# A hybrid encoder trunk in which the low halves of the second batch's output weights are multiplied first, its stores are cut in two, and three pauses of the planner are changed

## The chip, the cores and the metric

One Trainium2 chip, of which the kernel uses one core. The metric is the device time of one execution in microseconds (us). The core's engines each run their own list of instructions in order: TensorE (PE in the profile) multiplies and transposes, VectorE (DVE) and ScalarE (ACT) do element work, GpSimd (POOL) a few small powers, and SyncE (SP) issues nearly all DMA transfers. An instruction that waits holds up everything behind it on its engine.

## The reference

Two independent inputs (a prompt and a sample, 512 rows of 1024 columns each, fp32) go through one encoder layer and a final norm with the same weights:

```python
mod = c_act @ w_ada + b_ada                      # six vectors of 1024 per input: sh1 sc1 g1 sh2 sc2 g2
h = rms_norm(x, norm1_g) * (1 + sc1) + sh1
q_a, k_a, v_a, q_r, k_r, v_r, g_r = split(h @ w_in)
o_a = windowed_attention(q_a, k_a, v_a, sink)    # 8 heads of 64, window 128, distance bias, a sink
y = retention(q_r, k_r, v_r, decays)             # 4 heads of 128, both directions
yn = (y - mean(y)) * rsqrt(var(y) + EPS)         # per row and head
o_r = silu(g_r) * yn
x = x + g1 * (concat(o_a, o_r) @ w_out)
h = rms_norm(x, norm2_g) * (1 + sc2) + sh2
x = x + g2 * (square(relu(h @ w_mlp1)) @ w_mlp2) # 1024 -> 4096 -> 1024
return rms_norm(x, final_g)
```

Retention is evaluated as one 512 by 512 matrix of scores per head, multiplied by a table of decays. A reference of fp32 quality is wanted, so each fp32 product is made of three matmuls in the reduced type fp32r: both operands are split into a high part (a cast) and a low part (the difference), and high by high, high by low and low by high are added up in PSUM.

## The kernel before

**Stages.** A front part computes the first norm's modulations and the attention projections of batch 0 in an order that is written out step by step. Then `run_units` goes through a list of *units*. A unit loads a block of weights (a tile of 128x1024, 512 KB) and multiplies it. The next unit's load is called one unit ahead. The first list holds batch 0's retention values and, for each of four heads, the projections q, k and gate; the second list holds the same and attention for batch 1; the third is `out_units(0)`, the output projection of batch 0, and the fourth `out_units(1)`. An output projection has two column halves `hf` of 512, each with four units `kq` of 256 rows of the weight; its products `po_b_hf_t` are four banks, one for each tile `t` of 128 rows of x. After the mixing part come the two MLP matrices in a scheme of seven products (lines 840 to 1400).

**What runs between.** Each unit yields a few times, and at each yield `between` runs background work: a stage of an attention block or a retention head (`rate` stages per yield), the norm of batch 1's x, and a step of `background_mods` (`pace` steps per yield), which is 60 reductions `jka_b` on DVE for the rest of the six modulation vectors, each over a 128x1024 tile `raw_adat` loaded by SP. A retention head (`ret_head`) does scores `prs`, their decayed copies `rsf` and split `rsc`, values `py`, transposes `pyn`, row mean and variance on DVE, a power on POOL, a scaled copy `ryn` on ACT and transposes back `pyb`. A stage that yields n is not resumed until n yields later. What comes out of this Python order is then placed on the engines by a scheduler, so neighbours in the code may end up apart.

**Batch 1's output units.** Batch 0 splits each output weight itself and keeps both halves in DRAM (`kept_wo`); batch 1 loads the kept halves, `wh_wo1_hf_kq` and `wl_wo1_hf_kq`. The low halves go into a pool `late` that is opened after the mixing part's pool has been closed and lies over its memory. So the first of them may be loaded only after the last user of the old memory, which is the last `jka_b` reduction (`jka_b_3_7`) and its read of the accumulator. When a half `hf` is done, each tile is multiplied by the gate row (`go`) and added to x (`x2`); after the second half the tile is stored to DRAM (`x2s`, 512 KB), its squares are summed (`jk2`, ACT), the reciprocal root comes from POOL (`r2`), and the tile is scaled in place. The scaling waits for the store to have landed. Tiles 0 and 2 of batch 1 are scaled by ACT, tile 1 by DVE; tile 3 goes into copies `xl` and does not wait for its store. Then come transposes `px2`, which feed the first MLP's products `px_0_0_0` and `py_0_0_n`; some of those fill gaps between the output units.

The three matmuls of a product for the output units come from `mm3_late(groups, 1)`: for a group of two tiles or one, all high by high and high by low matmuls first, and then the matmuls with the low weight.

Of the kernel before, what the change touches and what calls it, by code (L numbers as in the profile page):

```python
# [12 lines left out]
AF = mybir.ActivationFunctionType  # L13
# [19 lines left out]
def trunk_kernel(ctx, tc, x0, x1, x0_t, x1_t, params, gate2_bias, w_ada_first, w_ada_t, w_ada_gate2, w_in_first, w_in,  # L33
# [34 lines left out]
    def small(shape, name, tag="small", bufs=24):  # L68
        return work.tile(shape, F32, tag=tag, name=name, bufs=bufs)
# [57 lines left out]

    def mm3_late(groups, late):

        for ps, lhs, rhs, start, _ in groups:  # L130
            nc.tensor.matmul(ps, lhs[0], rhs[0], start=start, stop=False)  # L131
            nc.tensor.matmul(ps, lhs[late], rhs[1 - late], start=False, stop=False)  # L132
        for ps, lhs, rhs, _, stop in groups:
            nc.tensor.matmul(ps, lhs[1 - late], rhs[late], start=False, stop=stop)  # L134

# [46 lines left out]
    def last_of(engine):  # L182
        return next(i for i in reversed(nc.cur_bb.bb.instructions) if i.engine == engine)
# [226 lines left out]
    def ret_head(b, h, q_, k_, v_, sg, mix):  # L410
# [41 lines left out]
        va = small([P, NT], f"rva_{nm}")  # L452
        nc.vector.tensor_scalar(va, mv[:, :, 1], EPS, None, ALU.add)
        nb = small([P, NT], f"rnb_{nm}")
        nc.vector.tensor_scalar(nb, mv[:, :, 0], -1.0, None, ALU.mult)
        rs = small([P, NT], f"rrs_{nm}")
        nc.gpsimd.tensor_tensor(rs, va, neghalf[:, :NT], ALU.pow)
        yn = f2(f"ryn_{nm}")
        nc.gpsimd.tensor_tensor(nb, nb, rs, ALU.mult)
        for t in range(NT):  # L460
            nc.scalar.activation(yn[:, t * P:(t + 1) * P], pn[:, t * P:(t + 1) * P], AF.Identity, bias=nb[:, t:t + 1],
                                 scale=rs[:, t:t + 1])
        yield 2
        pb = aux_bank(f"pyb_{nm}")
# [64 lines left out]
    def decay_table(b, h):  # L529
        if b == 1:  # L530
            dt = mwork.tile([P, TW], F32, tag="dtab", name=f"dtab_{b}_{h}", bufs=2)
            nc.sync.dma_start(dt, kept_tables[h])
            return dt
        dt = mwork.tile([P, TW], F32, tag="dtab", name=f"dtab_{b}_{h}", bufs=2)

        nc.scalar.activation(dt, dl, AF.Copy, scale=lg[:, 0, h:h + 1])
        nc.vector.scalar_tensor_tensor(dt, dl, nlb[:, h:h + 1], dt, ALU.mult, ALU.min)
        nc.scalar.activation(dt, dt, AF.Exp)
        nc.sync.dma_start(kept_tables[h], dt)
        return dt  # L540
# [176 lines left out]
    def out_units(b, late=None):  # L717
# [14 lines left out]

        def store(t):
            r0 = b * S + t * P
            nc.sync.dma_start(x2s[r0:r0 + P, :], x2[t])

# [16 lines left out]
        def unit(hf, kq):  # L753
# [20 lines left out]
            def use(wm):  # L774
# [3 lines left out]
                for ts_ in ((0,), (1,), (2,), (3,)) if kq == 3 else ((0, 1), (2, 3)):  # L778
                    mm3_late([(banks[hf][t], [ms[k][:, i, t * P:(t + 1) * P] for i in range(2)],
                               (w[0][:, k, :], w[1][:, k, :]), kq + k == 0, kq + k == 4) for t in ts_ for k in range(2)], 1)  # L780
                    if ts_[-1] == 1:
                        yield
                if kq == 3:
                    for t in range(NT):
# [4 lines left out]
                        nc.vector.tensor_tensor(g_, banks[hf][t], gr[hf], ALU.mult)  # L789
                        nc.vector.tensor_tensor(x2[t][:, hs], x2[t][:, hs], g_, ALU.add)  # L790
                        if hf == 1 and b == 1:
                            store(t)
                            squares(hf, t)
                            if t > 0:
                                scaled(t - 1)
# [408 lines left out]
    for h in range(RH):  # L1204
        units = units + ret_units(hT[0], 0, h)
    run_units(units, 1.3, {7: lambda: extra.append(norm_x1())})
    units = attn_units(hT[1], 1) + ret_v_units(hT[1], 1)
    for h in range(RH):
        units += ret_units(hT[1], 1, h)
    run_units(units, 1.3)  # L1210
    units, norm2_0 = out_units(0)
    run_units(units, 1.0)
    flush()
# [373 lines left out]
```

## Time and profile before

| what | value |
|---|---|
| time, median of 3 runs | 1107.09 us (1106.03 to 1108.5) |
| the profiled execution | 1107.0 us, of which 1105.2 us are its span |
| TensorE busy | 1081.8 us, 98% |
| VectorE busy | 864.2 us, 78% |
| ScalarE busy | 516.0 us, 47% |
| GpSimd busy | 53.3 us, 5% |
| read and written in HBM | 160.75 MB, 71.06 MB |
| mean granted TensorE clock | 0.998 |

The profile shows one execution. Its times are counted from the span's start. A row of a timeline has the start, the duration, the engine, the line, the operation, what is written and read, and in brackets the idle time before it with what ended it. In PE's rows durations overlap: the distance between starts is the pace. A DMA row of SyncE shows when the transfer was issued; how long it took to land stands in the view of DMA issues or in the chain of waits. The stages lie at about 0 to 56 us (front), 56 to 175 (batch 0), 175 to 345 (batch 1), 345 to 430 (`out_units(0)`), 430 to 505 (`out_units(1)` and the start of the first MLP matrix); after that come the MLPs.

### The profile page before, as it was taken

The numbers are of one execution on the slowest core, as the hardware profiler recorded it, in microseconds if no ns is written. First come the engines' busy times: TensorE is split into PE (matmuls) and PEld (weight loads), VectorE is DVE, ScalarE is ACT, GpSimd is POOL, SyncE is SP. The second block draws the span as 40 slices with busy tenths as digits, with TensorE's granted clock in tenths as the row PEclk, the third lists the DMA queues.
The fourth block names the chain that finished last, engine by engine and source line by source line (L and its number), as shares of the span: only waits on it lengthen the run. The fifth ranks groups of instructions, "written<-read, shape, count | busy, mean of one in ns | idle before, by whom it ended". The sixth has DMA issues, their size and how long they took to land.

```text
span 1105.2 us, 14046 instructions
## 1 busy us (share of the span) xinstructions
PE 1081.8 (98%) x5021; PEld 889.3 (80%) x5021; DVE 864.2 (78%) x1448; ACT 516.0 (47%) x885; POOL 53.3 (5%) x63
## 2 busy tenths in 40 slices
PE   8999999999999999999999999999999999999997
PEld 5777887777888787888888888888888888888886
DVE  7979898877885787789778777786759754589786
ACT  6576676545652443474433333333443732335342
POOL 1000000010000001000000000000000000002213
PEclk9999999999999999999999999999999999999999
DMA  9888898855545698633555445552883555525504
GB/s 373 336 303 314 303 346 271 248 179 175 171 156 180 229 362 302 256 146 126 190 181 184 159 152 176 169 190 105 300 325 109 187 192 196 206 77 191 190 20 152
DMA packets 86746, 232.73 MB, mean 211 GB/s; under 512 B 8578, under 2 KB 20882, under 8 KB 86676
## 3 DMA queue, kind: packets, MB, share of 16 engines
q1 hardware_dynamic: 86084, 231.25, 60.3%
q8 instruction: 39, 0.64, 0.2%
q10 hardware_dynamic: 432, 0.57, 0.1%
q14 instruction: 31, 0.25, 0.1%
q0 software_dynamic: 160, 0.02, 0.0%
HBM read 160.75 MB, written 71.06 MB: 210 GB/s over the span
## 4 chain that ended last, share of the span: by engine, by line
PE 82%; DVE 11%; ACT 2%; DMA 2%; issue 1%; POOL 1%; POOLq 0%; DVEq 0%; ACTq 0%
PE x L1357 16%; PE px_None L940 15%; PE y L1357 12%; PE py_None L940 11%; PE po L132 2%; PE po L134 2%; PE po L131 2%; DVE jka_b L178 2%; PE po L396 2%; PE ppt L389 1%; PE psc L360 1%; PE pj_rq L131 1%; PE pj_rq L132 1%; PE pj_rq L134 1%; DVE jka_f L178 1%
## 5 line engine op out<-in xcount | busy, mean ns | idle before, releaser
L1297 DVE TENSOR_TENSOR uc_l<-ur,uc_h 128x1024 fp32r<-128x1024 f32 x56 | 68.4, 1221 | 52.7 <-ACT uc_h L1297 35.5
L1357 PE MATMUL x<-wc_l,uc_h 128*128 128x512 f32 (+1 forms) x264 | 101.0, 383 | 0.0
L1357 PE MATMUL x<-wc_h,uc_l 128*128 128x512 f32 (+1 forms) x264 | 101.0, 383 | 0.0
L1357 PE MATMUL x<-wc_h,uc_h 128*128 128x512 f32 (+1 forms) x264 | 100.9, 383 | 0.0
L1297 ACT CAST uc_h<-ur 128x1024 fp32r<-128x1024 f32 x56 | 58.8, 1051 | 77.1 <-PE x L1357 25.1
L1357 PE MATMUL y<-wc_h,uc_h 128*128 128x512 f32 x192 | 74.7, 389 | 0.0
L1357 PE MATMUL y<-wc_l,uc_h 128*128 128x512 f32 x192 | 74.7, 389 | 0.0
L1357 PE MATMUL y<-wc_h,uc_l 128*128 128x512 f32 x192 | 74.7, 389 | 0.0
L1297 ACT CAST wc_h<-w 128x1024 fp32r<-128x1024 f32 x48 | 50.5, 1051 | 48.1 <-PE x L1357 24.7
L1297 DVE TENSOR_TENSOR wc_l<-w,wc_h 128x1024 fp32r<-128x1024 f32 x48 | 58.6, 1220 | 17.6 <-ACT wc_h L1297 13.6
L1357 PEld LDWEIGHTS x<-wc_h,uc_h 128*128 128x128 f32 x264 | 49.6, 188 | 9.9 <-issue 0.2
L1357 PEld LDWEIGHTS x<-wc_l,uc_h 128*128 128x128 f32 x264 | 49.6, 188 | 9.7
L1357 PEld LDWEIGHTS x<-wc_h,uc_l 128*128 128x128 f32 x264 | 49.6, 188 | 9.6
L131 PE MATMUL po<-wh_wo,ms 128*128 128x512 f32 x128 | 50.3, 397 | 0.0
L132 PE MATMUL po<-wh_wo,ms 128*128 128x512 f32 x128 | 49.8, 392 | 0.1
L178 DVE CUSTOM_DVE_ANT_0 jka_b<-raw_adat,cb,cols 128x1024 bf16<-128x1024 f32 x38 | 48.3, 1280 | 0.2
L845 ACT CAST wc_s4h<-raw_w 128x1024 fp32r<-128x1024 f32 x16 | 16.8, 1052 | 63.1 <-PE px_None L940 44.9
L370 ACT ACTIVATE st<-st,negm 128x256 f32<-128x256 f32 (+1 forms) x64 | 35.2, 554 | 20.1 <-DVE negm L365 20.1
L1357 PEld LDWEIGHTS y<-wc_h,uc_h 128*128 128x128 f32 x192 | 36.0, 188 | 7.5
L1357 PEld LDWEIGHTS y<-wc_l,uc_h 128*128 128x128 f32 x192 | 36.0, 188 | 7.5
L1357 PEld LDWEIGHTS y<-wc_h,uc_l 128*128 128x128 f32 x192 | 36.0, 188 | 7.5
L940 PE MATMUL py_None<-hch,wc_a 128*128 128x512 f32 x120 | 39.7, 389 | 0.0
(379 smaller groups left out, 2963.0 us busy)
## 6 DMA issues: line engine op xcount, KB each, us to landing
ur<-spill SPq DMA_DIRECT2D x56, 512.0 KB, 4.4
raw_adat<-in_w_ada_t_dram SPq DMA_DIRECT2D x36, 512.0 KB, 6.4
raw_w<-in_w_mlp_dram SPq DMA_DIRECT2D x32, 512.0 KB, 3.5
spill<-s SPq DMA_DIRECT2D x64, 256.0 KB, 3.6
w<-in_w_mlp_dram SPq DMA_DIRECT2D x32, 512.0 KB, 5.0
spill<-u SPq DMA_DIRECT2D x48, 256.0 KB, 2.0
raw_ada<-in_w_ada_t_dram SPq DMA_DIRECT2D x12, 512.0 KB, 9.3
x<-in_x_dram SPq DMA_DIRECT2D x12, 512.0 KB, 7.7
```

Source lines behind the costliest of these rows:

```text
L131: nc.tensor.matmul(ps, lhs[0], rhs[0], start=start, stop=False)
L132: nc.tensor.matmul(ps, lhs[late], rhs[1 - late], start=False, stop=False)
L134: nc.tensor.matmul(ps, lhs[1 - late], rhs[late], start=False, stop=stop)
L178: nc.vector.tensor_tensor_reduce(junk(f"jka_{name}_{sec}_{kc}_{b}"), t, cb[:, b, :], 1.0, bcol[:, sec * KC + kc:sec * KC + kc + 1] if bias ...
L360: nc.tensor.matmul(psc[:, :w], qs[hh][:, isl], k_[:, s, j0 * P:j1 * P], start=(s == 0), stop=(s == 1))
L370: nc.scalar.activation(st[hh][:, :w], st[hh][:, :w], AF.Exp, bias=negm[:, hh:hh + 1], scale=0.125, accum_out=den[:, hh:hh + 1])
L389: nc.tensor.transpose(pt[:, hh * P:(hh + 1) * P], st[hh][:, jj * P:(jj + 1) * P], ident)
L396: nc.tensor.matmul(po, va[:, j0 + jj, g].rearrange("p s e -> p (s e)"), pts[jj][:, s, :], start=(jj == 0 and s == 0), stop=(jj == nj - 1 a ...
L845: nc.scalar.copy(hi, src)
L940: self.last = nc.tensor.matmul(bank[:, cs], x[:, k, :], y, start=first and k == 0 and i == 0, stop=last and k == 3 and i == 2, skip_group_ ...
L1297: last_split[:] = [nc.scalar.copy(hi, src), nc.vector.tensor_sub(lo, src, f(hi))]
L1357: nc.tensor.matmul(out, left[n][x][:, i, ts_], right[n][y][:, i, cs], start=first and i == 0 and k == 0, stop=end and i == 1 and k == 2, s ...
```

## The change

```diff
@@ mm3_late
-        for ps, lhs, rhs, start, _ in groups:
-            nc.tensor.matmul(ps, lhs[0], rhs[0], start=start, stop=False)
-            nc.tensor.matmul(ps, lhs[late], rhs[1 - late], start=False, stop=False)
-        for ps, lhs, rhs, _, stop in groups:
-            nc.tensor.matmul(ps, lhs[1 - late], rhs[late], start=False, stop=stop)
+    def mm3_late(groups, late, low_first=False):
+        def low():
+            for ps, lhs, rhs, start, stop in groups:
+                nc.tensor.matmul(ps, lhs[1 - late], rhs[late], start=start and low_first, stop=stop and not low_first)
+        if low_first:
+            low()
+        for ps, lhs, rhs, start, stop in groups:
+            nc.tensor.matmul(ps, lhs[0], rhs[0], start=start and not low_first, stop=False)
+            nc.tensor.matmul(ps, lhs[late], rhs[1 - late], start=False, stop=stop and low_first)
+        if not low_first:
+            low()
@@ ret_head
-        nc.vector.tensor_scalar(va, mv[:, :, 1], EPS, None, ALU.add)
         nb = small([P, NT], f"rnb_{nm}")
         nc.vector.tensor_scalar(nb, mv[:, :, 0], -1.0, None, ALU.mult)
+        nc.vector.tensor_scalar(va, mv[:, :, 1], EPS, None, ALU.add)
...
-        yield 2
+        yield 3
         pb = aux_bank(f"pyb_{nm}")
@@ decay_table
-        nc.scalar.activation(dt, dl, AF.Copy, scale=lg[:, 0, h:h + 1])
+        with tc.issue_after(last_of(mybir.EngineType.Activation)):
+            nc.scalar.activation(dt, dl, AF.Copy, scale=lg[:, 0, h:h + 1])
@@ out_units
-        def store(t):
+        def store(t, cs=slice(0, D)):
             r0 = b * S + t * P
-            nc.sync.dma_start(x2s[r0:r0 + P, :], x2[t])
+            nc.sync.dma_start(x2s[r0:r0 + P, cs], x2[t][:, cs])
...
-                               (w[0][:, k, :], w[1][:, k, :]), kq + k == 0, kq + k == 4) for t in ts_ for k in range(2)], 1)
+                               (w[0][:, k, :], w[1][:, k, :]), kq + k == 0, kq + k == 4) for t in ts_ for k in range(2)], 1, b == 1)
...
+                        if b == 1:
+                            store(t, hs)
                         if hf == 1 and b == 1:
-                            store(t)
                             squares(hf, t)
@@ the body
-    run_units(units, 1.3, {7: lambda: extra.append(norm_x1())})
+    run_units(units, 1.3, {3: lambda: clock.__setitem__(3, 0.8), 7: lambda: extra.append(norm_x1())}, 0.0)
...
-    run_units(units, 1.3)
-    units, norm2_0 = out_units(0)
-    run_units(units, 1.0)
+    more, norm2_0 = out_units(0)
+    run_units(units + more, 1.3)
```

In words: batch 1's output units multiply with the low weight first and the high weight after it. The `x2` tiles of batch 1 are stored in halves of 256 KB, the first after `hf` 0. Each retention head pauses three yields in place of two between its row statistics and the transposes back, and computes the negated mean before the variance. The first step of a decay table is tied behind the last ACT instruction emitted so far. The background reductions rest during the first four units and then go at 0.8 per yield (0.7 before), and batch 1's units and `out_units(0)` are one list with one rate of 1.3, so that the first output weight is called for a unit earlier. PE, ACT, DVE and POOL execute as many instructions as before; SP issues four more transfers. The order on the engines changes in many places; the three on which the prediction rests follow.

**The start of batch 1's output units, SP and PE.** On SP, `wh_`/`wl_` are loads of the kept halves, `x2s` stores of batch 0's tiles. Before:

```order
L876 DMA raw_w1_0_0_4548<-in_w_mlp1_dram 128x1024
L119 DMA wl_wo1_0_0_4408<-kept_wo0_0_3901 128x1024
L119 DMA wh_wo1_0_0_4406<-kept_wo0_0_3901 128x1024
L119 DMA wh_wo1_0_1_4416<-kept_wo0_1_3972 128x1024
L119 DMA wl_wo1_0_1_4418<-kept_wo0_1_3972 128x1024
L119 DMA wl_wo1_0_2_4488<-kept_wo0_2_4025 128x1024
L735 DMA x2s_69<-x2_0_0_4139 128x1024
L735 DMA x2s_69<-x2_0_1_4144 128x1024
L735 DMA x2s_69<-x2_0_2_4149 128x1024
L735 DMA x2s_69<-x2_0_3_4154 128x1024
L119 DMA wh_wo1_0_2_4486<-kept_wo0_2_4025 128x1024
```

Now:

```order
L119 DMA wh_wo1_0_0_4406<-kept_wo0_0_3885 128x1024
L119 DMA wh_wo1_0_1_4416<-kept_wo0_1_3973 128x1024
L741 DMA x2s_69<-x2_0_0_4154 128x1024
L119 DMA wh_wo1_0_2_4486<-kept_wo0_2_4029 128x1024
L741 DMA x2s_69<-x2_0_1_4159 128x1024
L741 DMA x2s_69<-x2_0_2_4164 128x1024
L741 DMA x2s_69<-x2_0_3_4169 128x1024
L119 DMA wl_wo1_0_0_4408<-kept_wo0_0_3885 128x1024
L119 DMA wl_wo1_0_1_4418<-kept_wo0_1_3973 128x1024
L119 DMA wl_wo1_0_2_4488<-kept_wo0_2_4029 128x1024
```

The first low half `wl_wo1_0_0` stood ahead of the four stores of batch 0's tiles, and stands behind them now. On PE the first products of these units follow directly on the last product of `out_units(0)`, now:

```order
L132 MATMUL po_0_1_3_4193<-wl_wo0_1_3_4313,ms_0_3_0_4023 128x512
L132 MATMUL po_0_1_3_4193<-wl_wo0_1_3_4313,ms_0_3_1_4026 128x512
L132 MATMUL po_1_0_0_4426<-wl_wo1_0_0_4408,ms_1_0_0_4410 128x512
L132 MATMUL po_1_0_0_4426<-wl_wo1_0_0_4408,ms_1_0_1_4413 128x512
L132 MATMUL po_1_0_1_4427<-wl_wo1_0_0_4408,ms_1_0_0_4410 128x512
L132 MATMUL po_1_0_1_4427<-wl_wo1_0_0_4408,ms_1_0_1_4413 128x512
L136 MATMUL po_1_0_0_4426<-wh_wo1_0_0_4406,ms_1_0_0_4410 128x512
```

Before, the transposes `pyb_1_3` and eight products with `wh_wo1_0_0` stood between the first of these rows and the first use of `wl_wo1_0_0`.

**The last background reduction, DVE.** `jka_b_3_7` are the two reductions on whose end the load of `wl_wo1_0_0` waits. Before:

```order
L101 TENSOR_TENSOR wl_wo0_1_3_4286<-raw_wo0_1_3_4283,wh_wo0_1_3_4285 128x1024
L425 TENSOR_TENSOR rsc_1_3_3_4263<-rsf_1_3_3_4261,rsc_1_3_3_4263 128x512
L178 ISA jka_b_3_7_0_4278,mod_s1_90<-raw_adat_35_4201,cb_85,cols_82 128x1024
L178 ISA mod_s1_90 128x1
L178 ISA jka_b_3_7_1_4304,mod_s1_90<-raw_adat_35_4201,cb_85,cols_82 128x1024
L178 ISA mod_s1_90 128x1
L768 TENSOR_TENSOR ms_1_0_0_4410<-mix_1_0_2248,ms_1_0_0_4410 128x512
```

Now:

```order
L795 TENSOR_TENSOR go_0_1_2_4388<-po_0_1_2_4192,gate_0_0_512_4279 128x512
L795 TENSOR_TENSOR go_0_1_3_4391<-po_0_1_3_4193,gate_0_0_512_4279 128x512
L796 TENSOR_TENSOR x2_0_2_4164<-x2_0_2_4164,go_0_1_2_4388 128x512
L796 TENSOR_TENSOR x2_0_3_4169<-x2_0_3_4169,go_0_1_3_4391 128x512
L183 ISA jka_b_3_7_0_4394,mod_s1_90<-raw_adat_35_4331,cb_85,cols_82 128x1024
L183 ISA mod_s1_90 128x1
L183 ISA jka_b_3_7_1_4396,mod_s1_90<-raw_adat_35_4331,cb_85,cols_82 128x1024
L183 ISA mod_s1_90 128x1
L746 SCALAR_TENSOR_TENSOR v2_0_0_4451<-ss2_0_0_2113 128x1
```

The reductions have moved behind `go_0_1_3`, which reads the last product of `out_units(0)`, and behind two additions.

**The end of batch 1's output units, ACT.** `jk2` sums squares of a tile's second half, the rows that write `x2_1_t` scale a tile, `u` belongs to the MLP. Before:

```order
L730 ACTIVATE jk2_1_1_2_4891,ss2_1_2_4404<-x2_1_2_4662 128x512
L951 COPY u_0_2_4919<-px_0_0_0_4925 128x256
L730 ACTIVATE jk2_1_1_3_4902,ss2_1_3_4405<-x2_1_3_4667 128x512
L953 COPY u_0_3_4920<-py_0_0_3_4967 128x256
L749 ACTIVATE x2_1_2_4662<-x2_1_2_4662,r2_1_2_4906 128x1024
L821 ACTIVATE hr_1_0_4981<-px2_1_0_4985,mod_s1_90,mod_a1_88 128x512
```

Now:

```order
L736 ACTIVATE jk2_1_1_2_4895,ss2_1_2_4404<-x2_1_2_4664 128x512
L958 COPY u_0_2_4923<-px_0_0_0_4929 128x256
L960 COPY u_0_3_4924<-py_0_0_3_4971 128x256
L755 ACTIVATE x2_1_2_4664<-x2_1_2_4664,r2_1_2_4910 128x1024
L736 ACTIVATE jk2_1_1_3_4906,ss2_1_3_4405<-x2_1_3_4670 128x512
L828 ACTIVATE hr_1_0_4985<-px2_1_0_4989,mod_s1_90,mod_a1_88 128x512
```

The squares of tile 3 have moved behind the scaling of tile 2, which waits for tile 2's store. On PE, the products of `py_0_0_1` and `py_0_0_3` that stood between the last output product and the transposes `px2_1_0` (16 of them) now stand ahead of the last eight pairs of products with `wh_wo1_1_3`; the transposes of `x2_1_2` and `xl_1_0` stand where they stood.

1 line of the change is left out of this document (removed).

## The prediction

> **What bounds the kernel now.** I read PE's busy time by stage first (columns: window, length, busy time and count of PE, weight loads, DVE, ACT and POOL, granted clock, DMA share, GB/s), then the view of waits for PE between 53 and 510 us (us in total, times, longest).
>
> ```profile
> 56.00:505.00 449.00, 438.93 (x2156) 361.39 (x2155) 368.49 (x819) 244.87 (x518) 19.83 (x26) 1.00 0.70 242
> 505.00:1105.00 600.00, 592.75 (x2650) 490.91 (x2648) 447.00 (x536) 236.76 (x319) 29.98 (x29) 1.00 0.51 173
> ```
>
> ```profile
> PE pyb L466 <- ACT ryn L461: 3.1, 4, 1.3
> PE px L268 <- ACT x L749: 1.4, 1, 1.4
> PE pj_rq L131 <- DVE rv L298: 1.2, 1, 1.2
> PE py L124 <- ACT rsc L424: 1.0, 1, 1.0
> PE pj_rv L131 <- DVE ks L311: 0.8, 1, 0.8
> PE pj_rv L131 <- DVE qs L338: 0.8, 1, 0.8
> PE py L940 <- ACT wc_a L845: 0.7, 1, 0.7
> PE px L268 <- DVE x L751: 0.3, 1, 0.3
> ```
>
> PE sets the end. After 505 us the change leaves PE's work as it is. Between 56 and 505 us PE idles for 449.0 - 438.9 = 10.1 us, of which these rows hold 9.3. PE's products are the same in number, so **10.1 us is the most that can be won**, and each new wait of PE is paid in full. The question is which of these waits go, and which come.
>
> **What it wins.** The two waits for `ks` and `qs` (1.6 us) lie behind the first steps of two decay tables on ACT, which the order now puts later:
>
> ```profile
> 49.69 1.98 ACT L536 ACTIVATE dtab<-dl,lg 128x896 f32<-128x896 f32 x2 [1.67 <-DVE lg L523]
> ```
>
> 1.98 us of ACT covers 1.6 us of waiting: I take all of it, with 0 as the other end. The wait for `rv` (1.2) is DVE's, which ran a background reduction and a weight split just before it; the reductions now start later, and I take 1.2. The pause of three yields acts on the 3.1 us for `pyb`. Counting the order at PE's pace (below), the distance from `pyn` to `pyb` grows for heads 0 and 3 of batch 0 (7.0 to 8.2 and 4.1 to 8.4 us) but shrinks for heads 1 and 2 (5.4 to 4.3, 6.1 to 5.0), because the planner packs the other work differently; I take 0.6 of 3.1. The waits for `rsc` (1.0), `wc_a` (0.7) and the `x` of DVE (0.3) meet weights and splits that come earlier, or fall into the new wait below: 2.0. Together 1.6 + 1.2 + 0.6 + 2.0 = **5.4 us**, between 2 (only `ks` and one more go) and 8.7 (all rows but the 1.4, which gets its own term). Swapping the mean and the variance costs nothing: both are 0.16 us on an idle stretch of the same chain.
>
> **The first new wait: the low half of the first weight.** Now PE's first product for batch 1 reads `wl_wo1_0_0`, straight behind the last product of `out_units(0)`. That load waits for the read of the last reduction `jka_b_3_7`, and DVE now does the two reductions behind `go_0_1_3` and two additions, so behind that very last product. Before, they were done 9 us ahead. The rows (PE, SP, DVE, then the chain's transfer and two rows of DMA issues, the last number being the median us to landing):
>
> ```profile
> 428.69 0.39 PE L132 MATMUL po<-wh_wo,ms 128*128 128x512 f32 x1
> 428.92 0.62 PE L134 MATMUL po<-wl_wo,ms 128*128 128x512 f32 x2
> ...
> 432.14 1.08 PE L134 MATMUL po<-wl_wo,ms 128*128 128x512 f32 x4
> ```
>
> ```profile
> 421.32 0.32 SPq L119 DMA_DIRECT2D wl_wo<-kept_wo  x1
> ...
> 428.33 3.91 SPq L735 DMA_DIRECT2D x2s<-x  x4
> 432.33 0.84 SPq L119 DMA_DIRECT2D wh_wo<-kept_wo  x1
> ```
>
> ```profile
> 418.77 1.28 DVE L178 CUSTOM_DVE_ANT_0 jka_b<-raw_adat,cb,cols 128x1024 bf16<-128x1024 f32 x1
> ...
> 419.97 1.28 DVE L178 CUSTOM_DVE_ANT_0 jka_b<-raw_adat,cb,cols 128x1024 bf16<-128x1024 f32 x1
> ...
> 428.82 1.45 DVE L789 TENSOR_TENSOR go<-po,gate 128x512 f32<-128x512 f32 x2
> 430.19 1.28 DVE L790 TENSOR_TENSOR x<-x,go 128x512 f32<-128x512 f32 x2
> ```
>
> ```profile
> 431.50 7.75 DMA x2s<-x
> ```
>
> ```profile
> x2s<-x SPq DMA_DIRECT2D x4, 512.0 KB, 7.8
> ...
> kept_wo<-wh_wo SPq DMA_DIRECT2D x1, 512.0 KB, 2.7
> ```
>
> PE's pace is 0.23 us a product (428.69 to 428.92). Count from the last product's end, T0. DVE: `go` 0.7 (half of 1.45), two additions 1.28, two reductions of 1.28 with 1.2 between starts, 2.5: the load is issued at T0 + 4.5 at the earliest, 5.0 with the little that DVE lags. In an empty queue 512 KB take 2.7 us (the last row): **7.2 us** is the lower end. But SP has by then issued four stores of 512 KB and the load of `wh_wo1_0_2` in the 7 us before, and before, such a store took 7.75 us with a full queue; the first store went out at 428.33 and the last landed at 431.50 + 7.75 = 439.25, with two loads ahead of the four, 10.9 us for six transfers, 1.8 each. Six transfers from the first store (now at T0 - 1.7) at 1.8 land `wl_wo1_0_0` at T0 + 9.1; with the full 7.75 us from its own issue, T0 + 12.7. I take **9.0 us**, between 7.2 and 12.7, near the row of six transfers, since it has the same six. Nothing on PE can fill this: it goes in order. The second low half follows one transfer (1.8) later and PE needs it 5.4 us after the first (24 products of 0.23), so the wait is paid once.
>
> **The second new wait: the end of these units.** Low first means that every tile's last product is with the high weight, and 16 half-width products of the MLP now stand ahead of those. Rows before (PE; the chain of waits; DVE, ACT, POOL, DVE):
>
> ```profile
> 478.48 0.62 PE L134 MATMUL po<-wl_wo,ms 128*128 128x512 f32 x2
> ...
> 487.51 0.33 PE L268 MATMUL px<-ident,x 128*128 128x128 f32 x1 [1.39 <-ACT x L749]
> ```
>
> ```profile
> 482.50 3.71 DMA x2s<-x
> ...
> 486.31 1.16 ACT x L749
> ```
>
> ```profile
> 480.04 1.22 DVE L846 TENSOR_TENSOR wc_s4l<-raw_w,wc_s4h 128x1024 fp32r<-128x1024 f32 x1
> ```
>
> ```profile
> 484.65 0.63 ACT L730 ACTIVATE jk<-x 128x512 bf16<-128x512 f32 x1
> ```
>
> ```profile
> 485.64 0.55 POOL L742 TENSOR_TENSOR r<-v,neghalf 128x1 f32<-128x1 f32 x1 [0.40 <-DVE v L740]
> ...
> 486.22 0.88 DVE L747 TENSOR_SCALAR xl<-x,r 128x512 f32<-128x512 f32 x2 [0.66 <-POOL r L742]
> ```
>
> From the last product of tile 2 (478.5 + 0.5) to the transpose at 487.51 lie 8.5 us, of which 1.4 waits, so 7.1 of PE's own work. The order now leaves 2.3 us less: 16 half-width products at 0.11, and two tile-3 products at 0.23. The chain to the scaled tile 2: `wc_s4l` first waits for the last product of all (0.9) and takes 1.2; `go` and the addition 0.6 each; the store; the scaling 1.16. With 3.71 for the store that is 8.2, the same as the 8.5 of before, less whatever half the bytes save. So PE would wait 1.4 + 2.3 - 0.3 = 3.4 us there, or 2.4 with the shortest landing above (2.7). Then comes a second piece: the squares of tile 3 now stand behind that scaling on ACT, and after them the power and the copy: 0.63 + 0.2 + 0.55 + 0.44 + hops of 0.2 = 2.0 us before the next transposes, which were ready in time before. Together 4.4 to 5.4 in place of 1.4: I take **+3.0**, between +1.0 (both pieces hidden by a quicker store) and +4.0.
>
> The Trainium skill ("DMA: Bandwidth & Descriptors", the section on the anatomy of one DMA) gives a transfer about 2.0 us that do not depend on its size and the bytes at 436 GB/s: 512 KB to 256 KB would save 0.6 us of 3.2. By that the halves of the stores buy back 0.6 of the 3.0.
>
> **Smaller terms.** x of batch 1 is now loaded tile by tile between the half stores, each load behind the addition of the tile ahead, and the last weights stand behind them on SP. With landings of 2.7 to 3.7 us and 5 us of DVE work between two additions this fits, barely; the new order of the first retention heads has a few distances that shrink too. I take **+1.0**, between 0 and 3.
>
> **After a long idle PE may be slow.** At the start of the program, after 2.15 us without work and short bursts, transposes of 128 columns run at 0.235 us each (2.82/12) and 0.23 (3.68/16), later eight of them take 1.04:
>
> ```profile
> 2.15 2.82 PE L1125 MATMUL warm<-ident 128*128 128x128 f32 x12 [2.15 <-POOL ident masks.py:199]
> 5.88 3.68 PE L1014 MATMUL pcb<-ident,cact 128*128 128x128 f32 x16 [0.90 <-DVE cact L1003]
> ...
> 485.09 1.04 PE L268 MATMUL px<-ident,x 128*128 128x128 f32 x8
> ```
>
> The longest idle time later is 1.4 us and leaves no such trace. A wait of 9 us is more like the start: half pace over the 7.4 us that those two rows span would lose 3.7, none 0. I take the middle, **+1.8**.
>
> The Trainium skill ("TensorE: Matmul & The Clock Gate", Part 1) has a clock gate that halves PE's clock after about 3.4 us of idling and needs as long a busy time to lift it, an estimated loss of 1.7 us for each such gap. The start's rows agree in kind, though the granted clock of the profile reads 1.00 there.
>
> **The sum.** 1107.0 (the profiled execution, 1105.2 of span and 1.8 around it, 0.1 from the median of the three runs) - 5.4 + 9.0 + 3.0 + 1.0 + 1.8 = 1116.4: **1116 us**.
>
> **The rivals.**
> - *The tail holds.* The end of batch 1's units costs what it did, because the half stores land sooner. For it: 256 KB in place of 512. Against: the two orders above. 1116.4 - 3.0 = 1113.4.
> - *The queue of SP decides.* The loads of x and of the last output weights come late by a full queue's landing (7.75 in place of 3.7), once more 4 us: 1120.4. For it: the order on SP; against: DMA is less busy there.
> - *The first wait is not there.* If the low half lands by T0, because the scheduler's order is not what decides when the reductions run or the transfers are issued, the terms 9.0 and 1.8 fall away: 1107.0 - 5.4 + 4.0 = 1105.6, no change. With all 8.7 won and the tail holding, 1107.0 - 8.7 + 1.0 = 1099.3, faster. This side decides from where the wait behind `out_units(0)` is under 1.4 us (5.4 - 4.0). Against it stands that DVE, SP and PE each go in order.
> - *The edits do not do what they say*: the pause of three is one (heads 1 and 2 above), worth 0.6 either way.
>
> **Chances.** Forecast 0.5, tail 0.2, queue 0.15, no first wait 0.15 (0.07 faster, 0.06 same; the rest of it slower). A difference of 0.2%, 2.2 us, is about the least that a measurement of this kernel can tell. Faster 0.07, same 0.08 (0.02 from large wins in the tail's case), slower 0.85. The range reaches from 1107 (first wait 7.2, most of the wins, no slow pace) to 1122 (first wait 11, or the queue).
>
> **What would show it.** Right: one idle stretch of 7 to 12 us on PE behind the last `po` of `out_units(0)`, ended by a load of `wl_wo`; 4 to 5 us of waits at the `px` transposes at the end; no wait for `ks`, `qs` or `rv`; slower products right after the long wait. Wrong: that wait under 2 us, or `jka_b` ending well ahead of the last `go`.

## The result: 29 us slower, three times what was forecast

The changed kernel takes 1135.95 us (median of 4 runs, 1135.19 to 1137.87) against 1106.56 us for the kernel before (4 runs beside it). The ratio is 1.0265, with a 95% interval of 1.0249 to 1.0281: 29.4 us slower. The forecast was 1116 us, between 1107 and 1122. The direction was right; the size was not.

The profiled execution of the changed kernel took 1137.87 us, its span 1136.1 us, so 30.9 us more than the span before. First the two stages (columns as in the windows of before: window, length, busy time and count of PE, weight loads, DVE, ACT and POOL, granted clock, DMA share, GB/s), cut so that the second again holds the last 600 us:

```profile
56.00:536.00 480.00, 446.14 (x2154) 366.40 (x2153) 372.04 (x819) 247.06 (x521) 23.68 (x26) 0.98 0.66 227
536.00:1136.00 600.00, 592.88 (x2651) 491.01 (x2649) 446.99 (x536) 237.33 (x319) 29.91 (x29) 1.00 0.51 173
```

The second row is the one of before (592.75 busy of 600). The first stage has grown from 449 to 480 us. PE idles in it for 33.9 us where it idled 10.1, which is 23.8 of the 31. The other 7.2 is PE being busy longer with the same products (446.1 against 438.9): the granted clock now reads 0.98. Which waits they are (PE's view of waits between 56 and 530 us: us in total, times, longest):

```profile
PE po L132 <- DMA wl_wo<-kept_wo: 12.0, 1, 12.0
PE py L124 <- ACT rsc L429: 6.5, 4, 4.7
PE pyb L471 <- ACT ryn L466: 3.2, 3, 1.2
PE px L273 <- ACT x L755: 2.8, 2, 2.0
PE psc L365 <- ACT ryn L466: 1.8, 1, 1.8
PE pj_k L136 <- ACT h L292: 1.3, 2, 1.1
PE px L273 <- DVE xl L753: 1.3, 1, 1.3
PE rb L285 <- POOL r_x L1192: 1.1, 1, 1.1
PE py L125 <- DVE rsc L430: 1.0, 1, 1.0
PE py L947 <- DVE wc_s2l L853: 0.8, 1, 0.8
```

The rows for `rv` and `wc_a` are gone, and `ks` is down to 0.3, but rows have come that no row of before answers to: `psc`, `pj_k`, `rb`, and six times as much for `rsc`. Three stretches carry nearly all of it.

**Behind `out_units(0)`.** PE's timeline at the last product of batch 0 and the first of batch 1 (start, duration, and in brackets the idle time and what ended it):

```profile
441.49 0.61 PE L132 MATMUL po<-wl_wo,ms 128*128 128x512 f32 x2
454.15 2.04 PE L132 MATMUL po<-wl_wo,ms 128*128 128x512 f32 x4 [12.04 <-DMA wl_wo<-kept_wo]
455.99 0.63 PE L136 MATMUL po<-wh_wo,ms 128*128 128x512 f32 x1
456.42 0.63 PE L137 MATMUL po<-wh_wo,ms 128*128 128x512 f32 x1
```

This is the forecast wait, with 12.0 us. The chain of waits shows why, piece by piece, and SP's timeline what was in the queue ahead of the load:

```profile
444.08 1.28 DVE jka_b L183
445.37 1.20 DVE jka_b L183
446.64 7.27 DMA wl_wo<-kept_wo
```

```profile
439.99 0.32 SPq L741 DMA_DIRECT2D x2s<-x  x1
441.69 0.32 SPq L119 DMA_DIRECT2D wh_wo<-kept_wo  x1
442.10 2.41 SPq L741 DMA_DIRECT2D x2s<-x  x3
446.64 1.42 SPq L119 DMA_DIRECT2D wl_wo<-kept_wo  x3
```

PE's last product ends at about 442.1; the load goes out 4.5 us later, as counted, and lands 7.27 us after that, behind four stores and a load of 512 KB each. The landing is near the 7.75 us that was the upper end, not near the middle that was taken.

**In the middle.** The last product of `out_units(0)` now starts at 441.7 (the second of the row at 441.49) where it started at 429.1: before the wait above begins, the kernel is already 12.6 us late. Of that, 9.7 us are waits: the rows above that lie before 442 us, with five of 0.2 to 0.7, add up to 16.9 us, against 7.2 in the kernel before. Some 2 us more are slow products at 176 us (below). The largest is at 176 us (PE, ACT, DVE, then SP):

```profile
176.08 0.80 PE L124 MATMUL py<-rsc,rv 128*128 128x512 f32 x1 [4.71 <-ACT rsc L429]
177.83 0.79 PE L125 MATMUL py<-rsc,rv 128*128 128x512 f32 x1 [0.96 <-DVE rsc L430]
```

```profile
175.41 0.62 ACT L429 CAST rsc<-rsf 128x512 fp32r<-128x512 f32 x1 [8.93 <-DVE rsf L427]
```

```profile
173.48 1.28 DVE L183 CUSTOM_DVE_ANT_0 jka_b<-raw_adat,cb,onep 128x1024 bf16<-128x1024 f32 x1 [6.14 <-DMA raw_adat<-in_w_ada_t_dram]
```

```profile
160.20 2.98 SPq L159 DMA_DIRECT2D xt<-in_x_t_dram  x4
163.24 1.45 SPq L88 DMA_DIRECT2D raw_adat<-in_w_ada_t_dram  x2
```

Read from the last fence upwards: two background tiles are issued right behind the four loads of batch 1's x, 2 MB that stand ahead of them; DVE reaches a reduction whose tile has not landed and stands for 6.1 us, a wait that the kernel before does not have; `rsf` of a retention head is queued behind that reduction, ACT's `rsc` behind `rsf`, PE's `py` behind `rsc`. A background task holds up the foreground, because DVE goes in order.

**At the end.** ACT waits for the half store, does the squares of tile 3 only after the scaling, and PE waits twice (ACT, then PE):

```profile
513.16 1.15 ACT L755 ACTIVATE x<-x,r 128x1024 f32<-128x1024 f32 x1 [1.03 <-DMA x2s<-x]
514.21 0.62 ACT L736 ACTIVATE jk<-x 128x512 bf16<-128x512 f32 x1
```

```profile
514.36 0.66 PE L273 MATMUL px<-ident,x 128*128 128x128 f32 x4 [2.02 <-ACT x L755]
516.31 1.11 PE L273 MATMUL px<-ident,xl 128*128 128x128 f32 x4 [1.29 <-DVE xl L753]
```

The half store is shorter than the whole one, but ACT still waits for it. From the start of the last output product to this scaling it takes 6.25 us (506.91 to 513.16), as it did before (480.07 to 486.31, 6.24), and PE has less other work in between.

**Half pace.** Behind each of the three, PE's products are 0.43 us apart instead of 0.23 (455.99 to 456.42 above), and the windows show half a clock there:

```profile
176.00:181.00 5.00, 3.96 (x9) 2.77 (x10) 5.00 (x9) 4.82 (x9) 0.00 (x0) 0.50 1.00 405
454.00:457.50 3.50, 3.35 (x8) 2.70 (x9) 0.00 (x0) 0.00 (x0) 0.00 (x0) 0.50 1.01 384
517.00:522.30 5.30, 5.30 (x26) 5.30 (x26) 3.67 (x6) 3.64 (x6) 0.00 (x0) 0.50 0.00 0
```

PE was busy for 12.6 us in these at half pace, so some 6.3 us are lost: most of the 7.2 above.

### The profile page after: what moved, and what is told of

Its sections match the earlier page's. It is cut to its first block, busy times and chain, and to the rows that moved or that the text cites. A ratio compares the mean times of both kernels' runs of the same rounds, so it can differ in the third digit from the quotient of the medians.

```text
span 1136.1 us, 14044 instructions
## 1 busy us (share of the span) xinstructions
PE 1088.4 (96%) x5021; PEld 894.3 (79%) x5021; DVE 865.7 (76%) x1448; ACT 515.7 (45%) x885; POOL 57.1 (5%) x63
## 3 DMA queue, kind: packets, MB, share of 16 engines
q1 hardware_dynamic: 86660, 231.25, 58.9%
## 4 chain that ended last, share of the span: by engine, by line
PE 77%; DVE 13%; ACT 4%; DMA 3%; issue 2%; POOL 1%; SPq 0%; POOLq 0%; DVEq 0%; ACTq 0%
PE x L1363 15%; PE px_None L947 14%; PE y L1363 11%; PE py_None L947 11%; DVE jka_b L183 2%; PE po L401 1%; PE po L136 1%; PE po L132 1%; PE po L137 1%; PE psc L365 1%; PE ppt L394 1%; PE pj_rk L136 1%; DVE jka_f L183 1%; PE pj_rk L137 1%; PE pj_rq L136 1%
## 5 line engine op out<-in xcount | busy, mean ns | idle before, releaser
L1363 PEld LDWEIGHTS x<-wc_h,uc_h 128*128 128x128 f32 x264 | 49.6, 188 | 10.1 <-issue 0.4
L1363 PEld LDWEIGHTS x<-wc_l,uc_h 128*128 128x128 f32 x264 | 49.6, 188 | 9.8
L1363 PEld LDWEIGHTS x<-wc_h,uc_l 128*128 128x128 f32 x264 | 49.6, 188 | 9.6
L137 PE MATMUL po<-wh_wo,ms 128*128 128x512 f32 x128 | 50.4, 394 | 0.0
L132 PE MATMUL po<-wl_wo,ms 128*128 128x512 f32 x128 | 36.4, 401 | 12.0 <-DMA wl_wo<-kept_wo 12.0
```

Of the source, the lines that this page charges most:

```text
L132: nc.tensor.matmul(ps, lhs[1 - late], rhs[late], start=start and low_first, stop=stop and not low_first)
L1363: nc.tensor.matmul(out, left[n][x][:, i, ts_], right[n][y][:, i, cs], start=first and i == 0 and k == 0, stop=end and i == 1 and k == 2, s ...
```

## The experiments

Three questions had to be told apart: whether the wait behind `out_units(0)` is what the prediction said, which edits make the end slower, and which make the middle slower. "P" in the expectations is the prediction's mechanism, a last reduction that ends late, with what each expectation adds to it. Times are medians of 2 to 10 runs; the ratio is to the kernel before, run on the same chip, with its 95% interval. "Middle" is where the last product of `out_units(0)` starts, read from PE's timeline of one execution, less the 429.1 us of before; "units of batch 1" is the time from there to the last output product of all (50.9 us before, 65.2 in the change). In the change, its variants and the kernel with one list, the four transposes `pyb_1_3` stand ahead of that product instead of behind it, which is about 0.5 us of its lateness.

| kernel | time, us | ratio (95%) | middle | units of batch 1 |
|---|---|---|---|---|
| the change | 1135.95 | 1.0265 (1.0249 to 1.0281) | +12.6 | 65.2 |
| change without the new background pace | 1121.12 | 1.0126 (1.0096 to 1.0155) | +6.4 | 54.0 |
| change without low first | 1129.19 | 1.0199 (1.0167 to 1.0230) | +8.6 | 62.3 |
| before + background pace | 1121.94 | 1.0133 (1.0104 to 1.0163) | +5.5 | 58.9 |
| before + low first | 1106.13 | 0.9995 (0.9984 to 1.0007) | +0.2 | 48.2 |
| before + half stores | 1110.68 | 1.0044 (1.0028 to 1.0060) | -0.1 | 53.5 |
| before + low first and half stores | 1113.52 | 1.0062 (1.0040 to 1.0085) | -0.6 | 53.7 |
| before + one list of units | 1110.71 | 1.0033 (1.0022 to 1.0045) | +5.3 | 50.4 |
| before + pause of three | 1113.60 | 1.0057 (1.0034 to 1.0080) | +7.8 | 49.6 |
| before + decay tables tied | 1109.39 | 1.0024 (1.0015 to 1.0034) | +1.5 | 50.8 |
| before + low first and tables | 1108.16 | 1.0017 (1.0007 to 1.0027) | +2.5 | 48.0 |
| before + rest, then 1.0 | 1116.18 | 1.0086 (1.0066 to 1.0107) | +11.4 | 49.6 |
| before + 0.8 in the first list | 1111.12 | 1.0043 (1.0027 to 1.0059) | +7.1 | 49.6 |
| change + tiles two steps ahead | 1130.50 | 1.0217 (1.0200 to 1.0234) | +8.9 | 64.3 |
| change + 1.0 after the rest | 1128.35 | 1.0205 (1.0190 to 1.0220) | +14.8 | 52.5 |
| change + both | 1127.67 | 1.0194 (1.0179 to 1.0209) | +13.2 | 54.6 |

### What makes the wait behind `out_units(0)`

The change without the background's new pace:

```diff
-    run_units(units, 1.3, {3: lambda: clock.__setitem__(3, 0.8), 7: lambda: extra.append(norm_x1())}, 0.0)
+    run_units(units, 1.3, {7: lambda: extra.append(norm_x1())})
```

> The change with the background reductions' rest and rate undone (no rest, 0.7 per yield as before); all other edits stay. Theory P (the later reductions make both large waits: the 12.0 us for the low half, because the last reduction ends behind the last output product, and the 4.7 us behind the wait of VectorE for a late tile of the reductions): both waits go, with the slow products behind them, so 1136 - 14 - 8 = about 1114 us, PE's wait for a load of wl_wo under 2 us. Rival L (the low-first order makes the large wait whatever the reductions do): the wait for wl_wo stays at 8 us or more, and the time at 1128 us.

1121.12 us. The wait for `wl_wo` is gone and batch 1's units take 11.2 us less, as P says; that the time lies 7 us above P's figure is the middle, which the other edits leave 6.4 us late. The change with the high weight first again, as before (the call is shown; the helper is put back too):

```diff
-                               (w[0][:, k, :], w[1][:, k, :]), kq + k == 0, kq + k == 4) for t in ts_ for k in range(2)], 1, b == 1)
+                               (w[0][:, k, :], w[1][:, k, :]), kq + k == 0, kq + k == 4) for t in ts_ for k in range(2)], 1)
```

> The change with the low-first order undone (high by high and high by low first, as before); all other edits stay. Theory P: the load of wl_wo1_0_0 is as late as in the change and is now needed eight products (1.8 us) later, so PE still waits about 10 us for it; the waits at the transposes px at the end fall from 5.0 to about 1.5 to 3 us; 1136 - 2 - 3 = about 1131 us. Rival L: no wait for wl_wo, 1136 - 14 - 3 = about 1119 us.

1129.19 us: only 6.8 us of the 29 go, near P's 1131. The wait is still there, in pieces (PE's waits):

```profile
PE px L268 <- DVE x L752: 4.1, 4, 2.8
...
PE po L134 <- DMA wl_wo<-kept_wo: 0.8, 1, 0.8
```

PE first works through 16 products with the high weight, then meets transposes of batch 0's x2, which DVE scales only after the late reductions, and then the low weight. So it is the late reduction that makes the wait; low first joins the pieces and adds to their cost. The same from the other side, the two edits alone on the kernel before:

```diff
-    run_units(units, 1.3, {7: lambda: extra.append(norm_x1())})
+    run_units(units, 1.3, {3: lambda: clock.__setitem__(3, 0.8), 7: lambda: extra.append(norm_x1())}, 0.0)
```

> The kernel before with only the rest of four units and the rate of 0.8 for the background reductions. Theory P: PE waits about 10 us for wl_wo at the start of batch 1's output units, and VectorE's wait for a late tile in the middle costs PE 5 to 8 us: 1107 + 10 + 2 + 6 = about 1125 us. Rival L: no large wait for wl_wo, at most 1115 us.

1121.94 us, the dearest single edit: half of the whole loss. Its batch 1 units take 8.0 us longer, with `px` waiting 3.9 us for DVE and `wl_wo` 0.8, and its middle is 5.5 us late.

```diff
+        if low_first:
+            low()
...
+        if not low_first:
+            low()
```

> The kernel before with only the low-first order for batch 1's output units. Theory P: the last reduction ends early as in the kernel before, so the low half is there in time; only the waits at the px transposes at the end grow, by 2 to 4 us: 1109 to 1111 us. Rival L: a wait of 8 us or more for wl_wo, 1118 us or more.

1106.13 us, no difference (0.9984 to 1.0007). Low first alone costs nothing when the reductions are early; the 2 to 4 us that P gave it at the end did not come (`px` waits 1.7 us for ACT, 1.4 before).

The traces of all 17 kernels agree. In four of them the last reduction starts behind the last product of `out_units(0)`, by 3.4 to 5.6 us: in the change, in the change without low first, in the change with tiles two steps ahead, and in the kernel before with the background pace. In the other 13 it starts 8.7 us or more ahead, and PE waits for `wl_wo` by at most 0.3 us.

### What makes the end slower

Half stores alone, and with low first:

```diff
+                        if b == 1:
+                            store(t, hs)
                         if hf == 1 and b == 1:
-                            store(t)
```

> The kernel before with only the stores of batch 1's x2 tiles in halves. Theory H (the half stores make the growth at the end of batch 1's output units: each load of x now stands behind a store that waits for VectorE, and the transposes come nearer to the scaled tiles): PE's idle time between 475 and 525 us grows from 3 to 7 or 9 us, 1111 to 1113 us. Rival HL (it takes the low-first order as well; each alone is free): 1106 to 1108 us.

> The kernel before with the half stores and the low-first order. Theory H: like the half stores alone plus the second piece, the squares of tile 3 behind the scaling of tile 2 on ScalarE: 1113 to 1117 us. Rival HL: also 1113 to 1117 us, where the half stores alone stay at 1107. If neither piece matters: 1107 us.

1110.68 and 1113.52 us: 3.5 and 6.3 us more than the 1107.18 beside them, where low first alone made no difference. Theory H holds, if the first lies just under its range; rival HL does not, since the half stores alone are not free. PE's waits at the end (475 to 505 us) of the half stores alone, then of both:

```profile
PE px L268 <- ACT x L749: 2.2, 1, 2.2
```

```profile
PE px L273 <- ACT x L754: 3.0, 2, 2.2
PE px L273 <- DVE xl L752: 1.3, 1, 1.3
```

The second piece that the prediction saw, `xl` behind the scaling of tile 2, needs both edits. Behind these waits the granted clock reads 0.50, for 3.4 us (491.1 to 494.5) and for 6.8 us (490.4 to 497.2); the 1.4 us of before have no such trace. The store lands sooner than a whole one (3.71 us for tile 2's before). The row of the DMA issues of the changed kernel:

```profile
x2s<-x SPq DMA_DIRECT2D x8, 256.0 KB, 2.5
```

The 2.6 us that the prediction's source gives for 256 KB (the Trainium skill, "DMA: Bandwidth & Descriptors", the section on the anatomy of one DMA: 2.0 us and the bytes at 436 GB/s) are near this row, though that section is on transfers that GpSimd issues, and these are SP's. Its 3.2 us for 512 KB lie between two whole transfers of this case (2.7 and 3.71 us), so the 0.6 us saved are not settled by these rows. That the halves buy the end back does not hold.

### What makes the middle slower

The other edits, each alone on the kernel before. One list of units:

```diff
-    run_units(units, 1.3)
-    units, norm2_0 = out_units(0)
-    run_units(units, 1.0)
+    more, norm2_0 = out_units(0)
+    run_units(units + more, 1.3)
```

> The kernel before with only batch 1's units and out_units(0) in one list at one rate of 1.3. If the change without its pace edit (1121 us) is half stores with low-first (about 8 us) plus the rest, the list, the pause and the decay table hold about 6 us. Theory M (the one list packs the last heads closer): 2 to 4 us slower, with a wait of about 2 us for pyb near 425 us. Theory 0: within 1 us of 1107, the wait for rsc near 375 us gone.

1110.71 us, 3.5 more, as theory M gave. The wait for `rsc` is gone, as theory 0 expected, but `pyb` waits 5.7 us in six places (3.1 in four before; 1.4 of it at 426 us), and the middle is 5.3 us late.

```diff
-        yield 2
+        yield 3
```

(and the negated mean ahead of the variance)

> The kernel before with only the pause of three yields ahead of the transposes back, and the mean ahead of the variance. Theory M: within 1 us of 1107. Rival Y (the longer pause moves other stages onto the waits): 2 to 4 us slower, with waits for pyb that sum to 4 us or more (3.1 before). If the pause does what it is meant to: the pyb waits fall under 1.5 us, 1105 us.

1113.60 us. The pause does what it is for: `pyb` waits 1.7 instead of 3.1. But these rows are new (PE's waits):

```profile
PE po L131 <- ACT ms L767: 4.0, 1, 4.0
PE psc L360 <- ACT ryn L461: 1.9, 1, 1.9
...
PE po L131 <- DVE go L789: 1.4, 1, 1.4
```

These rows hold 7.3 us, against the 1.4 won, and behind two of them the granted clock reads 0.50, for 3.4 us from 251.3 and 6.8 us from 377.6. The reading is that a longer pause moves what follows it, so that the head's last pieces come later and PE meets other work that is not ready; the swap of mean and variance was not run by itself.

```diff
-        nc.scalar.activation(dt, dl, AF.Copy, scale=lg[:, 0, h:h + 1])
+        with tc.issue_after(last_of(mybir.EngineType.Activation)):
+            nc.scalar.activation(dt, dl, AF.Copy, scale=lg[:, 0, h:h + 1])
```

> The kernel before with only the decay table's first step tied behind ScalarE's last instruction. The prediction's term: both waits for ks and qs go, 1.6 us faster, 1105.5 us. Rival: as in the changed kernel's profile, where 1.0 of the 1.6 us are still there, 0.6 us faster or no difference.

> The kernel before with the two edits that have not cost anything by themselves: the low-first order and the decay table's tie. If their gains add up, 1.0 (low-first, 1106.1 against 1106.7 us) and 0.6 to 1.6: 1104.5 to 1106 us. If they are noise: 1107 us.

1109.39 and, with low first, 1108.16 us. The waits for `ks` and `qs` fall from 1.6 to 1.0, not to nothing, and waits for `h` (1.3), `r_x` (1.2) and `rk` (0.8) come. Slower by 2.3 and 1.1 us, not faster.

The background's pace, in two parts: the rest of four units with 1.0 per yield afterwards, and 0.8 in the first list with no rest:

```diff
-    run_units(units, 1.3, {7: lambda: extra.append(norm_x1())})
+    run_units(units, 1.3, {3: lambda: clock.__setitem__(3, 1.0), 7: lambda: extra.append(norm_x1())}, 0.0)
...
-    run_units(units, 1.3)
+    run_units(units, 1.3, {}, 1.0)
```

> The kernel before with the background reductions resting for the first four units and then going at 1.0 per yield in both lists, so that the last of them stands ahead of out_units(0)'s first additions. Theory P (the rest and the rate cost through when the last reduction ends): no wait for wl_wo and no large wait at the first px transposes, 1107 to 1113 us, what is left being VectorE's waits for late tiles. Rival R (the rest itself costs, in the middle, by tiles that come late): 1117 us or more, as with the rest and 0.8 (1122).

```diff
-    run_units(units, 1.3, {7: lambda: extra.append(norm_x1())})
+    run_units(units, 1.3, {7: lambda: extra.append(norm_x1())}, 0.8)
```

> The kernel before with the background reductions at 0.8 per yield in the first list and no rest. Theory P: they end earlier than before, so nothing new is late: 1105 to 1109 us. Rival R2 (the denser rate loads VectorE and the DMA queue more and costs by itself): 1112 us or more.

1116.18 and 1111.12 us, both between what the theories gave. In neither is there a wait for `wl_wo`, and in both the middle is late: by 11.4 us in the first, where `pyb` waits 7.0, and by 7.1 us in the second, with one new wait of 3.3 us, of the transposes `ppt` for ACT, at 151 us. A tenth of a step per yield more costs 4 us.

Slow products are part of these losses. Ahead of the last product of `out_units(0)` the granted clock reads 0.50 for 3.4 us with the background pace and with one list, for 6.8 us with 0.8 in the first list, for 10.2 us with the pause of three and with rest and 1.0; in the kernel before and with the tables alone it never does. With 0.8 it is the 6.8 us from 150.55 on, behind the wait of 3.3: PE is busy for 6.12 of them, so about 3 us are lost, as much as in the wait.

### Can the waits be taken away inside the changed kernel?

Two more edits, on the change: the background's tiles loaded two steps ahead of their reduction instead of one, and 1.0 instead of 0.8 steps per yield after the rest, which brings the last reduction ahead of the last `go`. Both rates hold in the first list alone; the second goes at 0.7, in the change as before.

```diff
         nxt = load(0)
+        nxt2 = load(1)
         yield
...
-            t, nxt = nxt, load(n + 1)
+            t, nxt, nxt2 = nxt, nxt2, load(n + 2)
```

> The change with the background tiles of the modulations loaded two steps ahead of their reduction in place of one. Theory Q (the middle lost most to one late tile: DVE stood 6.1 us for raw_adat, issued behind four loads of x, and PE then waited 4.7 + 1.0 us for rsc and ran about 1.5 us slower): that reduction no longer waits, PE's waits for rsc fall from 6.5 to under 2 us, and the time falls by 5 to 8 us, to 1128-1131. Theory O (the new order of the middle costs the time, whichever tile is late): another wait takes its place and the time stays at 1134-1138. The wait for wl_wo of 12 us stays in both.

1130.50 us, 5.5 less than the change. DVE has no wait for `raw_adat` any more, and PE's waits for `rsc` are down to 1.6. But `pyb` has grown:

```profile
PE po L132 <- DMA wl_wo<-kept_wo: 10.1, 1, 10.1
PE pyb L472 <- ACT ryn L467: 5.1, 3, 3.2
...
PE py L124 <- ACT rsc L430: 1.6, 2, 1.4
```

So the late tile is a cause, as theory Q says, and worth about 4 of the 12.6 us of the middle. The other 8.9 remain.

```diff
-    run_units(units, 1.3, {3: lambda: clock.__setitem__(3, 0.8), 7: lambda: extra.append(norm_x1())}, 0.0)
+    run_units(units, 1.3, {3: lambda: clock.__setitem__(3, 1.0), 7: lambda: extra.append(norm_x1())}, 0.0)
```

> The change with the background at 1.0 steps per yield after its rest in place of 0.8, so that the last reduction stands ahead of the last go of out_units(0) in DVE's order. Theory P (the wait behind out_units(0) is set by that reduction alone): no wait for wl_wo beyond 1 us and no slow products behind it, 12.0 + 1.9 us less, 1121-1124. Rival O (the denser background pushes as much into the retention heads): the wait goes too, but PE's other waits between 175 and 440 us grow, 1127 or more.

1128.35 us. The 12 us are gone and batch 1's units take 12.7 us less, but the time falls by 7.6 only. The middle is now 14.8 us late. `rsc` still waits 4.0, and `rq` is a wait that was not there (PE's waits):

```profile
PE pj_rq L136 <- DVE rq L303: 2.0, 1, 2.0
```

This is rival O's 1127 or more. Both edits together:

> Both of the edits before on the change: tiles two steps ahead and 1.0 steps per yield. If the two waits are separate causes (Q and P), both go: 1136 - 6 - 14 = 1116, 1113-1119. If the order decides (O), 1123 or more.

1127.67 us, 0.7 better than the second alone: the 5.5 and the 7.6 do not add up, as O says. Waits that are taken out of the middle come back at other places in it. Whether the new order puts them there or the denser background does, these runs do not separate. No version that was run beats the kernel before.

## Why the prediction was right on the sign and wrong on the size

Against its own execution the forecast added 9.4 us (1107.0 to 1116.4). The profiled execution added 30.9. Its terms:

- **What it wins, -5.4, with +1.0 for smaller terms: this is the step that failed.** It took PE's waits of before one by one and asked which would go. `rv` went, the 1.0 of `rsc` at its old place, `wc_a` and the 0.3 of `x` went, `ks` and `qs` fell by 0.6 of 1.6, and `pyb` did not fall (3.2): 3.8 of the 5.4 came. But the prediction did not ask what the new order puts in front of PE elsewhere, beyond 1.0 us for "smaller terms". The middle was forecast some 4 us shorter and became 12.6 us longer. The runs show that no edit to the middle's order is free: one list +5.3, the pause +7.8, the pace +5.5, the tables +1.5, even 0.1 more per yield +7.1. The prediction's own bounds (2 to 8.7 of wins, 0 to 3 of costs) left at most 1 us of loss. Even with every term at its dearest (wins 2, first wait 12.7, end 4.0, smaller terms 3, slow products 3.7) its sum comes to 1128.4, above its 1122 and still below the measured time.
- **The pause, 0.6 of 3.1.** Right in kind: alone it takes 1.4 off `pyb`, though with the other edits nothing is left of it. In the prediction it was worth 0.6 either way; alone it makes the kernel 6.4 us slower, through `ms`, `psc` and `go`.
- **The first new wait, +9.0.** Right in mechanism, place, and end of the chain; mis-sized. It measured 12.0: issue at T0 + 4.5 as counted, then 7.27 us to landing. The row of the full queue (7.75) was the right one; counting the six transfers from the first store at 1.8 each gave 4.6 for the landing and was too kind. The count was also off: SP's timeline of before has four loads ahead of the four stores, not two (`wh_wo` twice from 422.73, `wl_wo` twice from 424.01), which took 7.4 to 9.8 us to land. With 12.0 the wait lies inside the 7.2 to 12.7 given. What the runs add: low first, whose edit it seemed, is innocent alone; the late reductions are the cause.
- **The end, +3.0.** Both pieces came, in the order described: 2.8 at the scaled tiles, 1.3 at `xl` and 0.8 at `wc_s2l`, 4.9 in place of 2.4 (1.4, 0.7 and 0.3 before): +2.5. Half pace behind them costs 2.6 more, which had not been charged there.
- **Slow after a long idle, +1.8.** Right there: 3.35 us busy at half pace lose 1.7. But it happened three times, about 6.3 us in all, since the waits at 176 us and at the end bring it too. The prediction tied it to a wait of 9 us and took waits of 1.4 for harmless; what lies between was left out.
- **The rivals.** The tail did not hold, and the first wait was there. The loads behind the half stores did come in time: no row of PE's waits in batch 1's output units names them. The faster side's 8.7 us is a slip: the rows but the 1.4 add up to 7.9, and 8.7 is all of PE's idle time but the 1.4.

Added up: the middle some 16 us above the forecast (12.6 against 4 won), the first wait 3, the end 2, together 21 of the 21.5 us between forecast and profiled time.

The late tile is 4 of the middle's 12.6 us. What stays open is which neighbour in the new order makes each of the smaller waits. Single edits add 20 us there if summed (5.5 + 0.2 - 0.1 + 5.3 + 7.8 + 1.5), the change has 12.6; they interact, and only the late tile was tried for itself.

## What to carry to other kernels

When PE is 98% busy and a planner places the rest, its few waits are a sum over one order, and an edit that changes the order is not "these waits less"; it is a new draw, and around a well-fitted order the draws of this case all came out at or above it. Cost such an edit by the slack of the work it moves, with a loss as the likely end, and charge each new wait of some 2 us or more, and sometimes a shorter one, the slow products behind it. A background task in an in-order queue needs its operand well ahead: ask for each of its loads what was issued just before, and for its last step who waits for it.

## What the runs showed of the hardware

PE goes to half pace after far less idling than expected, and not by the length of one wait. In the kernel before with the pause of three, a single wait of 1.94 us is enough (the two products after it, 0.42 us apart):

```profile
251.28 1.01 PE L360 MATMUL psc<-ks,qs 128*128 128x384 f32 x2 [1.94 <-ACT ryn L461]
252.09 0.63 PE L131 MATMUL pj_rv<-wh_rv,h 128*128 128x512 f32 x1
252.51 0.63 PE L132 MATMUL pj_rv<-wh_rv,h 128*128 128x512 f32 x1
```

In the kernel before with the background's pace, a wait of 2.62 us is not; from 1.7 us after it the products are 0.23 apart again:

```profile
189.74 0.51 PE L124 MATMUL py<-rsc,rv 128*128 128x512 f32 x1 [2.62 <-ACT rsc L424]
```

The traces show what tells the two apart. Within each of the 17, all changes of the granted clock lie whole multiples of 3.41 us from each other. Cut along that grid, PE idles for 1.94 us of one window in the first case (3.41 less 1.47 busy), and the next window is at 0.50. The second wait is cut in two: 1.91 us of idling in one window, 0.93 in the next, and the clock stays at 1.00 (columns as above):

```profile
247.87:251.28 3.41, 1.47 (x8) 1.04 (x7) 2.98 (x10) 1.53 (x5) 1.74 (x2) 1.00 0.71 239
251.28:254.69 3.41, 3.41 (x9) 2.84 (x10) 0.62 (x2) 0.55 (x1) 0.00 (x0) 0.50 0.57 219
```

```profile
185.62:189.03 3.41, 1.50 (x8) 0.88 (x7) 2.50 (x4) 1.70 (x3) 0.00 (x0) 1.00 1.13 320
189.03:192.44 3.41, 2.48 (x9) 1.64 (x10) 2.73 (x5) 2.61 (x4) 0.00 (x0) 1.00 1.12 336
```

Over the 17 traces, 35 windows at full clock have 1.93 us of idling or more, and each is followed by one at 0.50. Of 53 with 1.3 to 1.92 us, five are (1.33 to 1.85 us). Full clock came back behind each of the 29 windows at 0.50 in which PE idled for 0.2 us at most, and behind none of the 15 with 0.7 us or more.

The Trainium skill ("TensorE: Matmul & The Clock Gate", Part 1) has a clock that is halved after an idle window of about 3.4 us, and the window runs freely. The halving agrees (0.43 and 0.23 us a product, a granted clock of 0.50), and so does the free-running window, by the grid of 3.41 us. That the window must be idle throughout does not: 1.93 us of idling in it were enough each time. So a wait of about 2 us costs nothing more, or an estimated 1.7 us more (half of 3.41) or a multiple of it, by where it falls.

The second surprise is the queue: a transfer of 512 KB that followed five others of that size within 7 us took 7.3 us, and the tile behind the four loads of x came only 10.2 us after its issue began (163.24 to 173.48), where a transfer of that size took 2.7 us with little ahead of it.
